# A bias table built in scratch memory: repeating the lines from on-chip memory, or from scratch memory itself

## The chip, the core and the metric

The kernel runs on one core of a Trainium2 chip. A core has TensorE (PE in the profile; its weight loads are PEld), VectorE (DVE), ScalarE (ACT), GpSimd (POOL) and SyncE (SP), each with an instruction stream of its own that it works off in order, and 16 DMA engines that carry the transfers which the others issue. SBUF is the on-chip memory of 128 partitions, PSUM the accumulators that PE writes. The metric is the device time of the whole program in microseconds (us).

## What is computed

One layer of a decoder trunk on 256 tokens of width 2048, in float32. The part that the change touches is the relative bias of the second head group:

```python
def reference(x, p, ln_mix_pre, w_in, ...):
    h = rms_norm(x, ln_mix_pre[i])
    q_sb, k_sb, v_sb, q_dl, k_dl, v_dl = split(h @ w_in[i])
    o_sb = stick_breaking_attention(q_sb, k_sb, v_sb)      # 8 heads
    o_dl = dilated_mixture(q_dl, k_dl, v_dl, rel_bias)     # 8 heads
    o = rms_norm(concat(o_sb, o_dl), ln_head[i])
    x = x + rms_norm(o @ w_out[i], ln_mix_post[i])
    g, u = split(rms_norm(x, ln_ffn_pre[i]) @ w_gate_up[i])
    x = x + rms_norm((silu(g) * u) @ w_down[i], ln_ffn_post[i])
    gate = sigmoid(rms_norm(x, ln_pli[i]) @ w_pli_gate[i])
    return x + gate * (p[i] @ w_pli_proj[i])

# in dilated_branch: logit[q, k] += rel_bias[t5_bucket(distance(q, k) * dilation)], per head
```

With 256 tokens the three dilations fold into one 128 x 256 bias per head that depends on query and key only by their distance: one line of 384 numbers per head, read one element further left in each row.

## The kernel before

Every large product is split in two float32r parts (`hi` and `lo`) and runs as three matmuls per 128 rows of weights, `hi*hi`, `hi*lo`, `lo*hi` (line 150). `load_w` brings 512 KB of weights at a time into one of four `wraw` buffers by a DMA that SyncE issues (line 99); ScalarE casts it to `whi` (line 104), VectorE takes the rest, `wlo` (line 105), both in five buffers. So weights are fetched several groups ahead, and a group is twelve matmuls on PE.

The attention works in four head groups of four: two of the stick-breaking kind, then two of the dilated kind. For each, `k`, `q` and `v` are projected (`project_T`, `project_v`); `project_T` evacuates (line 307), transposes on PE (line 312) into one of two `pt` accumulators, and ScalarE and VectorE split that into `kT` or `qT` (lines 318 and 319). The heads' own steps are put into the queue `pending`, one of which is written out per group of weights (`tick`): logits, sums, values (lines 353 to 355), `head_out` with a reciprocal root on POOL (`rsqrt`, line 201) and a scaling on VectorE (line 375), and the final transposes (line 380), which use the two `pt` accumulators as well. A scheduler puts the instructions of each engine into an order at build time; weights get a priority.

`load_bias` is called between the `k` and the `q` projection of the second stick group. A small matmul (line 471) and an addition (line 472) leave the eight lines in eight partitions of `line`, 384 numbers each. Line 474, on POOL's queue, writes each 128 times into `scratch` in DRAM; line 476 reads `scratch` back with a row step one element short, so that each row of `bias` is shifted by one. The first use of `bias` is line 438, in the first dilated group.

Of the kernel before, what the change touches and what calls it, by code (L numbers as in the profile page):

```python
# [10 lines left out]
F32 = mybir.dt.float32  # L11
# [5 lines left out]
P = 128  # L17
# [5 lines left out]
NH = 8  # L23
# [11 lines left out]
def kernel(  # L35
# [27 lines left out]
    nc = tc.nc  # L63
    x, p, w_in, w_out = x[0], p[0, 0], w_in[0], w_out[0]
    w_gate_up, w_down, w_pli_gate, w_pli_proj = w_gate_up[0], w_down[0], w_pli_gate[0], w_pli_proj[0]
    out = out[0]
# [4 lines left out]
    dram = ctx.enter_context(tc.tile_pool(name="dram", bufs=1, space=bass.MemoryType.DRAM))  # L71
# [53 lines left out]
    def later(fn, ready=lambda: True, first=False):  # L125
        (pending.appendleft if first else pending.append)((fn, ready))

    def after(n):
        at = clock[0] + n
        return lambda: clock[0] >= at  # L130
# [108 lines left out]
    with tc.tile_pool(name="mixed", bufs=1) as mixed:  # L239
# [46 lines left out]
        for j in (0, 2):  # L286
            nc.gpsimd.affine_select(
                out=zmask[:, j, :], in_=zmask[:, j, :], pattern=[[1, P]], base=-1, channel_multiplier=-1,
# [7 lines left out]
            out=tri[:, 0:P], in_=tri[:, 0:P], pattern=[[-1, P]], base=-1, channel_multiplier=1,  # L296
# [162 lines left out]
        def load_bias():  # L459

            oh = tmp.tile([P, 3 * P], F32, name="tmp")
            ac = tmp.tile([P, 3 * P], F32, name="tmp")
            line = tmp.tile([P, 3 * P], F32, name="tmp")
            rb = small.tile([32, NH], F32, name="rb", bufs=1)
            with tc.issue_after(mark[0]):
                nc.scalar.dma_start(out=oh[0:32], in_=onehot)
                nc.scalar.dma_start(out=rb, in_=rel_bias)
                nc.scalar.dma_start(out=ac[0:NH], in_=addc)
            def lines():
                pl = ps_a.tile([P, NB], F32, name="pa")  # L470
                nc.tensor.matmul(pl[0:NH, 0:384], lhsT=rb, rhs=oh[0:32], start=True, stop=True)
                nc.vector.tensor_tensor(line[0:NH], pl[0:NH, 0:384], ac[0:NH], ALU.add)
                scratch = dram.tile([NH, P, 384], F32, name="scratch")
                nc.gpsimd.dma_start(out=scratch, in_=line[0:NH].unsqueeze(1).broadcast_to([NH, P, 384]))
                skew = bass.AP(tensor=scratch.tensor, offset=scratch.offset + 127, ap=[[383, P], [P * 384, NH], [1, 2 * P]])
                nc.gpsimd.dma_start(out=bias, in_=skew)

            later(lines, after(4), first=True)
# [210 lines left out]
```

## Time and profile before

| | us |
|---|---|
| median of 3 runs (1289.17 to 1290.33) | 1289.73 |
| the profiled execution | 1289.67 |
| its span, first to last instruction | 1288.0 |
| PE busy in the span | 1264.1 (98%) |
| VectorE busy | 708.0 (55%) |
| ScalarE busy | 653.0 (51%) |
| POOL busy | 21.5 (2%) |

The span is what the profiler saw between the first and the last instruction; the execution's own time has 1.7 us more around it. Matmuls are pipelined and their ends are modelled, so PE's busy time says where it worked and not how well. A wait is put down to what released the engine last. A DMA's time to landing counts from its issue. The share of a DMA queue is the time of its packets over that of 16 engines in the stretch asked for.

### The profile page before, as it was taken

The numbers are of one execution on the slowest core, as the hardware profiler recorded it, in microseconds if no ns is written. First come the engines' busy times: TensorE is split into PE (matmuls) and PEld (weight loads), VectorE is DVE, ScalarE is ACT, GpSimd is POOL, SyncE is SP. The second block draws the span as 40 slices with busy tenths as digits, with TensorE's granted clock in tenths as the row PEclk, the third lists the DMA queues.
The fourth block names the chain that finished last, engine by engine and source line by source line (L and its number), as shares of the span: only waits on it lengthen the run. The fifth ranks groups of instructions, "written<-read, shape, count | busy, mean of one in ns | idle before, by whom it ended". The sixth has DMA issues, their size and how long they took to land.

```text
span 1288.0 us, 15227 instructions
## 1 busy us (share of the span) xinstructions
PE 1264.1 (98%) x5644; PEld 1018.6 (79%) x5644; DVE 708.0 (55%) x985; ACT 653.0 (51%) x1007; POOL 21.5 (2%) x39
## 2 busy tenths in 40 slices
PE   9999599999999999999999999999999999999998
PEld 6887488888888788888888888888888888887886
DVE  6575275555644755555555444455555545555754
ACT  7664255544543755555544334454554553445753
POOL 0001001000000000000000000000000000000000
PEclk9999799999999999999999999999999999999999
DMA  9856656555566666666666555666666665554662
GB/s 341 270 151 167 119 165 191 161 168 175 196 200 192 195 184 185 186 182 184 185 186 184 184 188 185 190 186 186 185 181 185 188 182 183 191 184 143 210 217 80
DMA packets 122811, 238.87 MB, mean 185 GB/s; under 512 B 7920, under 2 KB 8216, under 8 KB 122480
## 3 DMA queue, kind: packets, MB, share of 16 engines
q1 hardware_dynamic: 121360, 234.12, 59.0%
q0 software_dynamic: 1120, 3.67, 1.6%
q8 instruction: 44, 0.72, 0.2%
q14 instruction: 31, 0.25, 0.1%
q10 hardware_dynamic: 256, 0.10, 0.0%
HBM read 234.19 MB, written 3.67 MB: 185 GB/s over the span
## 4 chain that ended last, share of the span: by engine, by line
PE 96%; DMA 3%; DVE 0%; issue 0%; ACT 0%; POOL 0%; ACTq 0%; SPq 0%; DVEq 0%; POOLq 0%
PE pm L150 92%; DMA wraw<-in_w_in_dram 3%; PE pa L342 1%; PE pt L578 1%; PE pt L218 1%; PE pt L312 0%; PE pa L353 0%; PE pt L380 0%; PE pa L354 0%; PE pa L355 0%; PE pa L414 0%; ACT whi L104 0%; PE pt L450 0%; PE pa L416 0%; DVE wlo L105 0%
## 5 line engine op out<-in xcount | busy, mean ns | idle before, releaser
L150 PE MATMUL pm<-whi,hT_hi 128*128 128x512 f32 x1216 | 486.7, 400 | 0.8 <-ACT whi L104 0.8
L150 PE MATMUL pm<-whi,hT_lo 128*128 128x512 f32 x1216 | 481.7, 396 | 0.0
L150 PE MATMUL pm<-wlo,hT_hi 128*128 128x512 f32 x1216 | 481.3, 396 | 0.0
L110 DVE SCALAR_TENSOR_TENSOR wlo<-wraw,gT,whi 128x512 fp32r<-128x512 f32 x416 | 293.7, 748 | 242.9 <-ACT whi L109 242.7
L105 DVE TENSOR_TENSOR wlo<-wraw,whi 128x1024 fp32r<-128x1024 f32 (+1 forms) x222 | 269.8, 1216 | 276.0 <-ACT whi L104 275.3
L109 ACT ACTIVATE whi<-wraw,gT 128x512 fp32r<-128x512 f32 x416 | 278.6, 717 | 261.2 <-PE pm L150 258.2
L104 ACT CAST whi<-wraw 128x1024 fp32r<-128x1024 f32 (+1 forms) x222 | 231.2, 1042 | 313.7 <-PE pm L150 285.2
L150 PEld LDWEIGHTS pm<-whi,hT_hi 128*128 128x128 f32 x1216 | 228.7, 188 | 54.8 <-ACT whi L104 2.2
L150 PEld LDWEIGHTS pm<-whi,hT_lo 128*128 128x128 f32 x1216 | 228.4, 188 | 55.1
L150 PEld LDWEIGHTS pm<-wlo,hT_hi 128*128 128x128 f32 x1216 | 228.7, 188 | 53.0 <-DVE wlo L105 1.1
L150 PE MATMUL pm<-whi,fT_lo 128*128 128x512 f32 x352 | 139.4, 396 | 0.0
L150 PE MATMUL pm<-whi,fT_hi 128*128 128x512 f32 x352 | 139.4, 396 | 0.0
L150 PE MATMUL pm<-wlo,fT_hi 128*128 128x512 f32 x352 | 139.2, 396 | 0.0
L150 PEld LDWEIGHTS pm<-whi,fT_hi 128*128 128x128 f32 x352 | 66.1, 188 | 16.0
L150 PEld LDWEIGHTS pm<-wlo,fT_hi 128*128 128x128 f32 x352 | 66.1, 188 | 15.9
L150 PEld LDWEIGHTS pm<-whi,fT_lo 128*128 128x128 f32 x352 | 66.1, 188 | 15.9
L150 PE MATMUL pm<-whi,oT_hi 128*128 128x512 f32 x128 | 51.2, 400 | 0.0
L150 PE MATMUL pm<-whi,oT_lo 128*128 128x512 f32 x128 | 50.7, 396 | 0.0
L150 PE MATMUL pm<-wlo,oT_hi 128*128 128x512 f32 x128 | 50.6, 395 | 0.0
L150 PEld LDWEIGHTS pm<-whi,oT_lo 128*128 128x128 f32 x128 | 24.0, 188 | 5.7
L150 PEld LDWEIGHTS pm<-wlo,oT_hi 128*128 128x128 f32 x128 | 24.1, 188 | 5.5
L150 PEld LDWEIGHTS pm<-whi,oT_hi 128*128 128x128 f32 x128 | 24.1, 188 | 5.5
(119 smaller groups left out, 538.9 us busy)
## 6 DMA issues: line engine op xcount, KB each, us to landing
wraw<-in_w_gate_up_dram SPq DMA_DIRECT2D x176, 512.0 KB, 3.7
wraw<-in_w_in_dram SPq DMA_DIRECT2D x94, 512.0 KB, 3.8
wraw<-in_w_down_dram SPq DMA_DIRECT2D x88, 512.0 KB, 3.7
wraw<-in_w_out_dram SPq DMA_DIRECT2D x32, 512.0 KB, 3.7
wraw<-in_w_pli_gate_dram SPq DMA_DIRECT2D x32, 512.0 KB, 4.6
y_sb<-in_xT_dram SPq DMA_DIRECT2D x8, 256.0 KB, 6.7
y_sb<-in_x_dram SPq DMA_DIRECT2D x4, 512.0 KB, 7.5
x_sb<-in_x_dram SPq DMA_DIRECT2D x4, 512.0 KB, 6.5
```

What stands on the lines that cost most here:

```text
L104: nc.scalar.copy(hi[:, sl], raw[:, sl])
L105: nc.vector.tensor_tensor(lo[:, sl], raw[:, sl], hi[:, sl].bitcast(F32), ALU.subtract)
L109: nc.scalar.activation(out=hi[:, c], in_=raw[:, c], func=AF.Copy, scale=g)
L110: nc.vector.scalar_tensor_tensor(out=lo[:, c], in0=raw[:, c], scalar=g, in1=hi[:, c].bitcast(F32), op0=ALU.mult, op1=ALU.subtract)
L150: nc.tensor.matmul(self.pm[t], lhsT=a[:, g * KG + c, t, :], rhs=b[:, c, :], start=g == 0 and c == 0 and a is a_hi and b is hi, stop=g * KG ...
L218: nc.tensor.transpose(out=pt[:, k * P:(k + 1) * P], in_=x_sb[:, t, (c * 4 + k) * P:(c * 4 + k + 1) * P], identity=ident)
L342: nc.tensor.matmul(out, lhsT=a[u], rhs=b[w], start=i == 0, stop=i == 2)
L578: nc.tensor.transpose(out=pt[:, k * P:(k + 1) * P], in_=s[t][:, k * P:(k + 1) * P], identity=ident)
```

## The change

The eight lines are first written once to a small piece of DRAM, `lines_d` (12 KB). A second transfer reads `lines_d` 128 times into `scratch`, from DRAM to DRAM. `scratch` is laid out as 128 rows of eight lines instead of eight blocks of 128 rows, so that the repetition is the outermost dimension of both sides; the strides of the skewed read follow. All three transfers stand on POOL's queue, and each waits for the one before it to land.

```diff
-                scratch = dram.tile([NH, P, 384], F32, name="scratch")
-                nc.gpsimd.dma_start(out=scratch, in_=line[0:NH].unsqueeze(1).broadcast_to([NH, P, 384]))
-                skew = bass.AP(tensor=scratch.tensor, offset=scratch.offset + 127, ap=[[383, P], [P * 384, NH], [1, 2 * P]])
+                lines_d = dram.tile([1, NH * 384], F32, name="lines_d")
+                scratch = dram.tile([P, NH * 384], F32, name="scratch")
+                nc.gpsimd.dma_start(out=lines_d.rearrange("o (h i) -> (o h) i", h=NH), in_=line[0:NH])
+                nc.gpsimd.dma_start(out=scratch, in_=lines_d.broadcast_to([P, NH * 384]))
+                skew = bass.AP(
+                    tensor=scratch.tensor, offset=scratch.offset + 127,
+                    ap=[[NH * 384 - 1, P], [384, NH], [1, 2 * P]])
                 nc.gpsimd.dma_start(out=bias, in_=skew)
```

The new transfers change the order that the scheduler gives to some instructions; all that moves beside POOL's queue lies around the values of the second stick group. On POOL, from the last root of the first stick group on, before:

```order
L201 TENSOR_TENSOR rs_970<-d_968,mhalf 128x2
L474 DMA scratch<-tmp 1024x1x384
L201 TENSOR_TENSOR rs_1564<-d_1562,mhalf 128x2
L201 TENSOR_TENSOR rs_1596<-d_1594,mhalf 128x2
L476 DMA bias<-scratch 128x8x256
L201 TENSOR_TENSOR rs_1628<-d_1626,mhalf 128x2
L201 TENSOR_TENSOR rs_1660<-d_1658,mhalf 128x2
```

and after (`rs` are the roots of one head each, `d` what they are taken of; `tmp` is `line`):

```order
L201 TENSOR_TENSOR rs_970<-d_968,mhalf 128x2
L475 DMA lines_d<-tmp 8x384
L476 DMA scratch<-lines_d 128x3072
L480 DMA bias<-scratch 128x8x256
L201 TENSOR_TENSOR rs_1566<-d_1564,mhalf 128x2
L201 TENSOR_TENSOR rs_1598<-d_1596,mhalf 128x2
L201 TENSOR_TENSOR rs_1630<-d_1628,mhalf 128x2
L201 TENSOR_TENSOR rs_1662<-d_1660,mhalf 128x2
```

The read of `bias` has moved ahead of the first two of the group's four roots, and one DMA more stands there. On VectorE, behind the last addition of the second stick group's sums (line 417), the roots' users (line 375) and the sums under them (line 367), before:

```order
L367 TENSOR_SCALAR d_1562<-ssh 128x2
L105 TENSOR_TENSOR wlo<-wraw,whi 128x1024
L367 TENSOR_SCALAR d_1594<-ssh 128x2
L105 TENSOR_TENSOR wlo<-wraw,whi 128x1024 x4
L319 TENSOR_TENSOR kT<-pt,kT 128x4x128
L105 TENSOR_TENSOR wlo<-wraw,whi 128x1024
L319 TENSOR_TENSOR kT<-pt,kT 128x4x128
L375 TENSOR_SCALAR tmp<-pa,rs_1564 128x128 x2
L375 TENSOR_SCALAR tmp<-pa,rs_1596 128x128 x2
```

and after:

```order
L367 TENSOR_SCALAR d_1564<-ssh 128x2
L375 TENSOR_SCALAR tmp<-pa,rs_1566 128x128 x2
L105 TENSOR_TENSOR wlo<-wraw,whi 128x1024
L367 TENSOR_SCALAR d_1596<-ssh 128x2
L375 TENSOR_SCALAR tmp<-pa,rs_1598 128x128 x2
L105 TENSOR_TENSOR wlo<-wraw,whi 128x1024
L367 TENSOR_SCALAR d_1628<-ssh 128x2
L375 TENSOR_SCALAR tmp<-pa,rs_1630 128x128 x2
```

Each scaling now stands right behind the sum whose root it uses, one head after the other. On PE the values (lines 353 to 355) of the third and fourth of these heads, which stood side by side, have moved ahead accordingly, with twelve matmuls of line 150 between heads.

## Rows read from the trace of the kernel before

**Rows 1.** From the page: PE's busy time, granted clock and memory traffic in 40 slices.

```profile
PE 1264.1 (98%) x5644; PEld 1018.6 (79%) x5644; DVE 708.0 (55%) x985; ACT 653.0 (51%) x1007; POOL 21.5 (2%) x39
PEclk9999799999999999999999999999999999999999
GB/s 341 270 151 167 119 165 191 161 168 175 196 200 192 195 184 185 186 182 184 185 186 184 184 188 185 190 186 186 185 181 185 188 182 183 191 184 143 210 217 80
```

**Rows 2.** Waits of PE, whole span: who waited for whom, total us, times, longest.

```profile
PE pt L380 <- DVE qT L319: 15.6, 1, 15.6
PE pm L187 <- DVE junk L184: 1.3, 1, 1.3
```

**Rows 3.** Chain that ended last, 95 to 240 us: start, length, what.

```profile
106.91 0.22 PE pt L380 x2
...
127.66 28.71 DMA wraw<-in_w_in_dram
...
159.43 0.69 PE pt L380 x2
160.11 4.34 PE pm L150 x12
...
165.09 2.85 PE pm L150 x12
```

**Rows 4.** ScalarE's timeline, 127 to 160 us: start, length, what, [idle before <- releaser].

```profile
152.92 1.04 ACT L104 CAST whi<-wraw 128x1024 fp32r<-128x1024 f32 x1 [19.33 <-DMA wraw<-in_w_in_dram]
156.47 1.04 ACT L104 CAST whi<-wraw 128x1024 fp32r<-128x1024 f32 x1 [2.50 <-DMA wraw<-in_w_in_dram]
157.42 0.58 ACT L318 CAST qT<-pt 128x512 fp32r<-128x512 f32 x1
```

**Rows 5.** DMA issues, windows 117:120 (two rows), 127:130: count, KB, us to landing.

```profile
scratch<-tmp POOLq DMA_DIRECT2D x1, 1536.0 KB, 35.5
wraw<-in_w_in_dram SPq DMA_DIRECT2D x1, 512.0 KB, 3.7
...
wraw<-in_w_in_dram SPq DMA_DIRECT2D x1, 512.0 KB, 28.7
```

**Rows 6.** DMA queues, 123 to 152 us: packets, MB, share of 16 engines.

```profile
q0 software_dynamic: 667, 1.46, 47.0%
q1 hardware_dynamic: 879, 1.69, 18.1%
```

**Rows 7.** Busy time by engine, then PE's clock, DMA share, GB/s, behind the stall.

```profile
159.50:163.50 4.00, 4.00 (x11) 3.23 (x12) 3.13 (x4) 1.25 (x2) 0.00 (x0) 0.51 0.73 210
```

**Rows 8.** POOL's DMA queue and its one issue, 198 to 212 us.

```profile
q0 software_dynamic: 272, 1.05, 23.1%
...
bias<-scratch POOLq DMA_DIRECT2D x1, 1024.0 KB, 8.5
```

**Rows 9.** Memory traffic in 40 slices and POOL's DMA queue, 427 to 440 us (`gpost`).

```profile
GB/s 0 0 0 0 0 328 76 302 403 454 403 429 328 403 233 113 214 372 422 290 69 0 0 0 0 0 0 0 0 0 0 95 82 88 277 410 410 208 44 88
...
q0 software_dynamic: 144, 1.05, 22.5%
```

**Rows 10.** POOL's timeline, 110 to 240 us.

```profile
119.95 1.28 POOL L474 DMA_DIRECT2D scratch<-tmp  x1 [13.31 <-DVE tmp L472]
194.45 0.71 POOL L201 TENSOR_TENSOR rs<-d,mhalf 128x2 f32<-128x2 f32 x1 [73.22 <-DVE d L367]
...
198.54 0.95 POOL L476 DMA_DIRECT2D bias<-scratch  x1
```

**Rows 11.** A small DMA load, from the list of issues.

```profile
rb<-in_rel_bias_dram ACTq DMA_DIRECT2D x1, 1.0 KB, 2.4
```

**Rows 12.** First use of `bias`, VectorE's timeline, 185 to 245 us.

```profile
239.95 0.29 DVE L438 CUSTOM_DVE_ANT_0 tmp<-pa,bias 128x128 f32<-128x128 f32 x1 [1.02 <-PE pa L342]
```

**Rows 13.** Waits of VectorE, 100 to 350 us.

```profile
DVE wlo L105 <- ACT whi L104: 87.5, 59, 19.7
...
DVE tmp L375 <- POOL rs L201: 8.1, 11, 0.9
```

## The prediction

> **What bounds the kernel now.** I read the page first. The granted clock is at its upper level in all slices but one, and the engine that is nearly always busy is TensorE (PE), so a gain has to be found where PE stands still or runs at the lower clock [rows 1]. Then the waits of PE over the whole span: one stands out, 15.6 us before the transposes of line 380, put down to VectorE's `qT` of line 319; the next longest is 1.3 us [rows 2]. Then the chain of waits in that stretch, to see what stood behind VectorE. It is a weight load: issued at 127.66 us, landed 28.71 us later, at 156.37, and the transposes follow at 159.43 [rows 3]. The link between them is ScalarE, which works in order: its evacuation of `qT` (157.42) stood queued behind two casts, at 152.92 and 156.47, whose weights had not landed; the first had waited 19.33 us [rows 4].
>
> Why did the weights not land? The load issued between 117 and 120 us lands in 3.7 us, the one issued between 127 and 130 takes 28.7 us. What lies between is the repetition of the bias lines, `scratch<-tmp`, issued at 119.95 and 35.5 us under way [rows 5, 10]. While it ran (123 to 152 us), its queue held 47.0% of the 16 DMA engines' time, which is 7.5 engines busy without a break, and the weights got 18.1% [rows 6]. Its source is 8 partitions of SBUF, each read 128 times, and 7.5 of 16 fits eight engines with one head each. A weight load lies on all sixteen and is not there until its last engine has delivered; so eight clogged engines delay every load.
>
> The Trainium skill, "DMA: Bandwidth & Descriptors", section "Rules for kernel authors", says that an outermost dimension smaller than 16 confines a transfer to at most that many engines. The 47.0% agrees with it.
>
> PE's stop also has an echo: the page's clock row dips in the stall's own slice, the fifth [rows 1], and in the four microseconds in which PE works again the granted clock is 0.51 [rows 7]. That is the lower level, 1.2 GHz, after a stretch in which PE did nothing.
>
> **The change part by part.**
>
> *What goes.* The stall of 15.6 us [rows 2]. The lower clock behind it: the two transposes took 0.69 us and take 0.22 elsewhere, twelve matmuls took 4.34 and the next twelve 2.85, so 0.47 + 1.49 = 2.0 us [rows 3]. Together 17.6 us, if no new wait takes the place.
>
> *How much delay the loads bear.* The load on the chain landed at 156.37 and PE lost 15.6 us, so it may land as late as 156.37 - 15.6 = 140.8 and cost nothing. It is issued at 127.66 and lands in 3.7 us when nothing is in its way, at 131.4. So 9.4 us of delay are free; each further microsecond costs PE one. The load ahead of it bears more in the same way.
>
> *The first hop.* The 12 KB go out by a transfer of their own: about 1 us of issue on POOL, which does nothing from 120 to 194 us [rows 10], and a landing that I bound by the 1 KB load, 2.4 us, and by the 1 MB load that POOL issues, 8.5 us [rows 8, 11]. It is nearer to the small one; the repetition is issued at some 123 instead of 120 us. Nobody waits for the `bias` before the additions at 239.95 us [rows 12], so the hop costs nothing on PE.
>
> *The repetition itself.* Memory to memory is not in this trace. What counts is how long it holds each engine, S, because a load can be delayed by at most that. Three rows bound it, each spread over 16 engines. The `gpost` load reads one line of 8 KB 128 times from memory: 22.5% of 13 us is 2.9 us for 1.05 MB, so 4.4 us for 1.57 MB [rows 9]. The `bias` load, read in 1 KB runs: 23.1% of 14 us is 3.2 us, so 4.8 [rows 8]. The old repetition: 47.0% of 29 us is 13.6 us for 1.46 MB, so 14.7 for all of it [rows 6]. I take 4.6, near the first two: the new source is memory, a line of 12 KB read 128 times, which is what `gpost` does; only the target differs. Then the load lands at 131.4 + 4.6 = 136.0, 4.8 us early. At 14.7 it lands at 146.1, 5.3 us late.
>
> *The `bias` load.* It moves from 198.54 us to right behind the repetition, around 133. There it meets a prefetch that has lost ground. If all its 3.2 us fell before the same load, that would land at 139.2, still 1.6 us early. Where it stands now it costs PE nothing either: no wait of PE but the stall is over 1.3 us, and its 8.5 us make none [rows 2, 8]. So moving it gives and costs 0, as long as S is below 6 us; beyond that it comes after the load in question.
>
> *What the move holds up on POOL.* The order puts both new DMAs and the `bias` DMA ahead of all four reciprocal roots of the second stick group, and POOL waits in order for the repetition to land. The first of the four ran at 194.45 [rows 10], with the stall gone at 176.9. Even a repetition that takes 35.5 us from 123 is done at 159. So nothing waits; it would only do so from a repetition of over 53 us.
>
> *The new order on VectorE and PE.* Each head's scaling (line 375) now follows its root directly, and the products of heads 2 and 3 stand with twelve matmuls between them instead of side by side. VectorE then waits up to 0.9 us for each root, as it does now, with the next `wlo` queued behind: 4 x 0.9 = 3.6 us at worst, but VectorE waits for ScalarE's casts (87.5 - 19.7) / 58 = 1.2 us at each `wlo` of that stretch anyway [rows 13]. The instructions on PE are the same in number. I take 0, with 0.3 us either way.
>
> **Sum.** The profiled execution took 1289.67 us (span 1288.0), the median of the runs is 1289.73; the two agree. 1289.67 - 15.6 - 2.0 = 1272.1.
>
> **The rivals.**
>
> *A smaller stall stays.* Two mechanisms end in this. The repetition keeps its pace per byte but over 16 engines: S = 14.7, 5.3 us late, 1277.4, or 1279.4 if the lower clock comes back with it. Or memory carries it twice, read and write: 3.15 MB beside weights at 185 GB/s. The best slices that the trace shows are 454 GB/s in one of a third of a microsecond [rows 9] and 341 in one of the page's forty [rows 1], so S is 3.15/(454 - 185) = 11.7 us or 3.15/(341 - 185) = 20.2 us, the load lands 2.3 or 10.8 us late, and the time is 1274.4 to 1282.9, with the clock 1284.9. For it speaks that the target is memory too; against it that 454 GB/s passed for reading alone without a sign of a limit.
>
> The Trainium skill, "HBM Reference", section "Specifications (TRN2)", gives about 358 GB/s per core. By it S would be an estimated 18.2 us and the time some 1281 to 1283; the 454 GB/s of the trace speak against so low a limit for a core that runs alone.
>
> *It doesn't spread, and is slower.* If the repetition stays on eight engines at the old pace, everything is as before but starts a hop later: 1.28 us of issue and 2.4 of landing [rows 10, 11]. The load then lands at 160.1, the stall is 19.3 us and the time 1293.4. More generally, the kernel is slower from the point where S passes 156.37 - 131.4 = 25 us. For it: the eight engines are my reading of a share, not a row that names them. Against it: in the new transfer 128 is the outermost size on both sides.
>
> *No change*: S happens to lie between 22 and 28 us. No row points there.
>
> **How the numbers follow.** I give the forecast 0.62, the smaller stall 0.26 (0.10 for the old pace over 16 engines, 0.16 for memory that carries it twice), no change 0.05, slower 0.07. A measurement of this kernel tells some 0.2% from no change, 2.6 us; both of the first two cases but for a sliver are faster by more. So faster 0.88, same 0.05, slower 0.07. The range: from 1271.0 (the 0.3 us of the order and a little for a stall removed more fully) up to 1279.8, which takes in S = 14.7 with its clock and about two thirds of the smaller-stall case: 0.62 + 0.17 = 0.79.
>
> **What would show it.** Right: PE's wait before line 380 is gone; the loads issued from 124 to 130 us land in under 13 us; the clock's row has no dip in the fifth slice; the two new queue entries land by about 135 us, and `bias` is issued then. S can be read as the share of POOL's queue times the length of its window. Wrong: loads that still take over 13 us, with PE idle behind them (then S is what I mis-sized); or POOL's roots late around 177 us and PE waiting behind line 375; or a new wait of PE between 135 and 150 us with the `bias` load beside it.

## The result, and the profile after

| | before | after |
|---|---|---|
| median of 4 runs each, us | 1289.76 | 1271.37 (1271.30 to 1271.86) |
| ratio, 95% interval | | 0.9858 (0.9841 to 0.9875) |
| span of the profiled execution, us | 1288.0 | 1269.7 |
| PE busy | 1264.1 (98%) | 1261.5 (99%) |

The kernel is 18.4 us faster; 17.6 were forecast, 1272.1 us, and the range of 1271.0 to 1279.8 holds the time. The page of the kernel after, for [rows 1]: the clock's row has no dip any more.

```profile
PE 1261.5 (99%) x5644; PEld 1017.2 (80%) x5644; DVE 708.7 (56%) x985; ACT 652.8 (51%) x1007; POOL 21.5 (2%) x40
PEclk9999999999999999999999999999999999999999
```

Waits of PE in the whole span, for [rows 2]. The 15.6 us before line 380 are gone, and what was second is now first:

```profile
PE pm L187 <- DVE junk L184: 1.3, 1, 1.3
PE pm L150 <- DVE wlo L105: 0.5, 1, 0.5
```

POOL's timeline, for [rows 10]: the hop, the repetition, the read of `bias`, and the first root of the second stick group.

```profile
119.47 0.71 POOL L475 DMA_DIRECT2D lines_d<-tmp  x1 [13.30 <-DVE tmp L472]
121.73 0.57 POOL L476 DMA_DIRECT2D scratch<-lines_d  x1 [1.54 <-DMA lines_d<-tmp]
132.10 0.93 POOL L480 DMA_DIRECT2D bias<-scratch  x1 [9.81 <-DMA scratch<-lines_d]
176.43 0.71 POOL L201 TENSOR_TENSOR rs<-d,mhalf 128x2 f32<-128x2 f32 x1 [43.40 <-DVE d L367]
```

The DMA issues, for [rows 5]: the three of POOL, and the two weight loads issued as the repetition began, at 123.95 us (window 122 to 124) and 127.17 us (window 127 to 130).

```profile
scratch<-lines_d POOLq DMA_DIRECT2D x1, 1536.0 KB, 10.1
...
bias<-scratch POOLq DMA_DIRECT2D x1, 1024.0 KB, 9.1
...
lines_d<-tmp POOLq DMA_DIRECT2D x1, 12.0 KB, 2.0
...
wraw<-in_w_in_dram SPq DMA_DIRECT2D x1, 512.0 KB, 9.0
...
wraw<-in_w_in_dram SPq DMA_DIRECT2D x1, 512.0 KB, 7.3
```

The loads beside the repetition now take 7 to 9 us instead of 28. The repetition held POOL's queue for this share of the 16 engines in 122 to 132 us:

```profile
q0 software_dynamic: 144, 1.57, 49.6%
```

Share times 16 engines times length of the window is the engine time, what a single engine would need for all packets: 0.496 x 16 x 10 = 79 us, 5.0 us on each of 16. For the kernel before the same row over 121 to 156 us is

```profile
q0 software_dynamic: 704, 1.58, 42.1%
```

which is 0.421 x 16 x 35 = 236 us of engine time for as many bytes. The start and length of each packet in the two traces bear out the number of engines that the prediction read from a share: before, up to eight packets of the repetition are under way at once (eight for 20.2 us, nine for less than 0.1); after, up to sixteen (more for 0.2 us). So the engines were not only fewer, each of them was three times as slow. The prediction had this pace only as an upper bound of S (14.7 us against 4.4 and 4.8) and did not ask where it comes from; the experiments below do.

### The profile page after: what moved, and what is told of

Its sections match the earlier page's. It is cut to its first block, busy times and chain, and to the rows that moved or that the text cites. A ratio compares the mean times of both kernels' runs of the same rounds, so it can differ in the third digit from the quotient of the medians.

```text
span 1269.7 us, 15227 instructions
## 1 busy us (share of the span) xinstructions
PE 1261.5 (99%) x5644; PEld 1017.2 (80%) x5644; DVE 708.7 (56%) x985; ACT 652.8 (51%) x1007; POOL 21.5 (2%) x40
## 3 DMA queue, kind: packets, MB, share of 16 engines
HBM read 235.76 MB, written 3.68 MB: 189 GB/s over the span
## 4 chain that ended last, share of the span: by engine, by line
PE 98%; DMA 1%; DVE 0%; issue 0%; ACT 0%; POOL 0%; ACTq 0%; DVEq 0%; POOLq 0%
PE pm L150 94%; PE pa L342 1%; PE pt L582 1%; PE pt L218 1%; PE pt L312 1%; DMA wraw<-in_w_in_dram 0%; DMA gT<-in_gains_dram 0%; PE pa L353 0%; PE pa L354 0%; PE pa L355 0%; PE pt L380 0%; PE pa L414 0%; PE pt L450 0%; PE pa L416 0%; DVE wlo L105 0%
```

## The experiments

Each run was timed against the kernel before on the same chip. Each row of POOL's DMA queue (packets, MB, share of 16 engines) is asked for from before the repetition's first packet to behind its last.

### Memory to memory, but with 8 outermost

```diff
-                scratch = dram.tile([P, NH * 384], F32, name="scratch")
+                scratch = dram.tile([NH, P, 384], F32, name="scratch")
-                nc.gpsimd.dma_start(out=scratch, in_=lines_d.broadcast_to([P, NH * 384]))
+                nc.gpsimd.dma_start(
+                    out=scratch,
+                    in_=lines_d.rearrange("o (h i) -> (o h) i", h=NH).unsqueeze(1).broadcast_to([NH, P, 384]))
```

(The strides of the skewed read go back to those of the kernel before.)

> Memory to memory as in the changed kernel, but scratch laid out as eight blocks of 128 rows again, so that 8 is the outermost size of the repetition. POOL's order is the old one here (bias behind two roots). The changed kernel takes 1271.4 us; its repetition has 128 packets of 12 KB. If the spread over 16 engines alone made the gain (eight engines at the old pace, S = 29 us), the stall is back: 1288 to 1294. If what was slow is the reading of one SBUF partition per engine, the new pace on eight engines gives S = 2 x 4.9 = 9.9 us, the load lands 0.5 us too late at most, and the time is 1271.4 to 1273. If the new order of the roots made the gain, it is lost with the old order: 1289.

Measured: 1271.43 us (1271.10 to 1271.93), as fast as the changed kernel. POOL's queue, 122 to 136 us:

```profile
q0 software_dynamic: 704, 1.58, 30.6%
```

0.306 x 16 x 14 = 69 us of engine time, 8.6 us on each of eight engines, where the second theory has 9.9. So 128 as the outermost dimension, the part of the change that looked like its core, is not needed for the gain. And the order of the roots isn't either: in this run `bias` is read at 180.33 us, behind two of the roots, as before.

### From SBUF, but from 128 partitions

```diff
-                nc.tensor.matmul(pl[0:NH, 0:384], lhsT=rb, rhs=oh[0:32], start=True, stop=True)
-                nc.vector.tensor_tensor(line[0:NH], pl[0:NH, 0:384], ac[0:NH], ALU.add)
+                nc.vector.tensor_copy(
+                    rb16.rearrange("b (h r) -> b h r", r=16), rb.unsqueeze(2).broadcast_to([32, NH, 16]))
+                nc.tensor.matmul(pl[:, 0:384], lhsT=rb16, rhs=oh[0:32], start=True, stop=True)
+                nc.vector.tensor_tensor(line, pl[:, 0:384], ac, ALU.add)
...
-                nc.gpsimd.dma_start(out=scratch, in_=line[0:NH].unsqueeze(1).broadcast_to([NH, P, 384]))
+                nc.gpsimd.dma_start(
+                    out=scratch.rearrange("h (r j) i -> (h r) j i", j=8),
+                    in_=line.unsqueeze(1).broadcast_to([P, 8, 384]))
```

(`ac` is loaded with 16 copies of each line.)

> No hop and no memory source: the matmul of the lines makes 16 copies of each line in 128 partitions (its left side is widened), and one transfer from SBUF writes each partition eight times. So 16 engines, source SBUF as before. If the spread is what counts and the pace of the SBUF source is better too with 8 partitions per engine, S is about 5 us and the time 1271.4, or a little less. If the old pace per engine stays (14.7 us on each of 16), the load lands 5.3 us late: 1276.7, with the clock up to 1278.7.

Measured: 1271.61 us (1271.01 to 1272.35). POOL's queue, 119 to 127 us, and the repetition's landing, without a hop ahead of it:

```profile
q0 software_dynamic: 368, 1.57, 53.7%
...
scratch<-tmp POOLq DMA_DIRECT2D x1, 1536.0 KB, 7.8
```

0.537 x 16 x 8 = 69 us again. So SBUF as a source is not slow in itself, and the detour through memory is not needed either. What both runs share, against the kernel before, is that the repeated reading doesn't go to partitions 0 to 7 alone.

### The slack: the repetition done twice and three times

```diff
+                for i in range(2):
+                    spare = dram.tile([P, NH * 384], F32, name=f"spare{i}")
+                    nc.gpsimd.dma_start(out=spare, in_=lines_d.broadcast_to([P, NH * 384]))
                 nc.gpsimd.dma_start(out=scratch, in_=lines_d.broadcast_to([P, NH * 384]))
```

(`range(1)` for twice.)

> The changed kernel with the repetition done twice (the first into a spare piece of memory that nobody reads), back to back. By the slack of 9.4 us: S = 2 x 4.9 = 9.9 us, the load lands 0.5 us late, 1271.4 to 1272. If the slack was overestimated and the 4.9 us are already at its edge: a stall of some 5 us, 1276. If engines' time is not what delays the loads (for example the hop or a port that the sources share), nothing changes: 1271.4.

> The same with three repetitions. By the slack: S = 14.9 us, 5.5 us late, a stall of some 5.5 us and 1277, up to 1279 if the clock falls with it. If engines' time is not what delays the loads: 1271.4.

Measured: 1272.01 us (1271.35 to 1273.20) with two, 1279.58 (1279.18 to 1279.81) with three. With two the load issued at 127.05 us lands after 13.1 us and PE waits 0.8 us for its weights. With three the old stall is back in small. Waits of PE, whole span, of the kernel with three repetitions:

```profile
PE pt L380 <- DVE qT L319: 5.9, 1, 5.9
PE pm L187 <- DVE junk L184: 1.3, 1, 1.3
```

and its chain, 115 to 165 us:

```profile
126.78 19.07 DMA wraw<-in_w_in_dram
...
148.90 0.69 PE pt L380 x2
149.59 4.56 PE pm L150 x12
...
154.78 2.85 PE pm L150 x12
```

5.5 us of stall were expected and 5.9 came; the clock adds (0.69 - 0.22) + (4.56 - 2.85) = 2.2 us, and 5.9 + 2.2 = 8.1 is nearly all of the 8.2 us between 1271.4 and 1279.6. So the term "9.4 us of delay are free, each further one costs PE one" holds. Three repetitions also move three times the bytes in memory, so by themselves they don't show that the loads wait for engines and not for memory. The kernel before shows that: there the loads waited longest, while all queues together moved 107 GB/s (122 to 154 us).

### Which eight partitions: 0, 4 to 28; 0, 2 to 14; 0, 16 to 112

The transfer of the kernel before, SBUF to memory, eight engines, one source partition each. Only the step between the partitions differs; the matmul makes as many copies of each line as the step says, and one of them is read (here 4; in the other two runs 2 and 16).

```diff
-                nc.gpsimd.dma_start(out=scratch, in_=line[0:NH].unsqueeze(1).broadcast_to([NH, P, 384]))
+                nc.gpsimd.dma_start(
+                    out=scratch, in_=line[0:32:4].unsqueeze(1).broadcast_to([NH, P, 384]))
```

> The transfer of the kernel before, eight engines and SBUF as source, no hop; only the eight source partitions are no longer 0 to 7 but 0, 4, 8 to 28 (the matmul makes four copies of each line and every fourth partition is read). In the run e1_mem8 a packet of 4608 B from memory took 191 ns on eight engines, in the kernel before 681 ns from partitions 0 to 7. If it was slow because one engine reads one partition over and over, nothing changes: 681 ns a packet, 1290. If it was slow because neighbouring partitions are read through one port, these eight have a port each: about 200 ns, S = 8.6 to 9.9 us, 1271.4 to 1272.

> The same with source partitions 0, 2, 4 to 14. If one partition per engine is what is slow: 1290, 681 ns a packet. If ports of four neighbouring partitions are: four ports instead of two, so half of 681, 340 ns a packet, S = 14.6 us on eight engines; the load lands 0.5 to 5.3 us late, 1272 to 1279.

> The same with source partitions 0, 16, 32 to 112. If only the distance between them counts, this is the best of the three: 200 ns, 1271.4 to 1272. By the port table of the Trainium skill, SBUF - State Buffer, Door 1, these eight lie on four ports, as those of e6_step2 do: an estimated 340 ns a packet and the time of e6_step2.

Measured: 1271.76 us (1271.19 to 1272.88) with a step of 4, 1273.70 (1272.76 to 1274.36) with 2, 1274.24 (1273.20 to 1275.72) with 16. POOL's queue with a step of 4, 122 to 136 us:

```profile
q0 software_dynamic: 704, 1.58, 28.9%
```

with a step of 2, 121 to 139 us:

```profile
q0 software_dynamic: 704, 1.58, 37.8%
```

and with a step of 16, 122 to 141 us:

```profile
q0 software_dynamic: 704, 1.58, 37.8%
```

In engine time 65, 109 and 115 us, where partitions 0 to 7 took 236. It isn't that one engine reads one partition over and over, for that is so in all four. It isn't the distance either, for a step of 16 is no better than one of 2. What fits is that neighbouring partitions share a way out, a port: with a step of 1 the eight sources lie in two groups of four neighbours, with a step of 2 in four, with a step of 4 in eight, and the first doubling of the groups doubles the pace, the second makes it 1.7 times as fast again. By its pace a step of 16 counts as four groups, so partitions far apart would share a port as well; that was foretold from the table named next, and no run here tries a single pair of them.

The Trainium skill, "SBUF — State Buffer", section "Door 1: The DMA port swizzle", gives the table: partitions 0 to 3 on one port, 4 to 7 on another, and of 0, 16 to 112 always two on one. It puts a port at 27.2 GB/s. The measured rates agree: 1.58 MB in 29.5 us of eight engines is 54 GB/s on two ports, in 14.4 us 110 GB/s on four (step of 16). With eight ports it is 195 GB/s in 8.1 us, about what eight engines do from memory (8.6 us), so there the ports need no longer be the limit.

### Sixteen engines on neighbouring partitions

```diff
+                nc.gpsimd.dma_start(
+                    out=scratch.rearrange("h (r j) i -> (h r) j i", j=64),
+                    in_=line[0:16].unsqueeze(1).broadcast_to([16, 64, 384]))
```

(Two copies of each line, in partitions 0 to 15, in place of the transfer of the kernel before.)

> Sixteen engines, but neighbouring sources: two copies of each line in partitions 0 to 15, each written 64 times, 16 the outermost size. If engines were the limit (14.7 us of each at the old pace of 681 ns) or if four ports are (two engines share what one had: again 681 ns), S is 14.7 us on all 16 and the load lands 4 to 5.3 us late: 1275 to 1279. If 16 engines alone help: 200 ns a packet, 1271.4.

Measured: 1276.93 us (1275.89 to 1278.98). POOL's queue, 122 to 140 us, and the repetition's landing:

```profile
q0 software_dynamic: 368, 1.57, 81.8%
...
scratch<-tmp POOLq DMA_DIRECT2D x1, 1536.0 KB, 19.2
```

0.818 x 16 x 18 = 236 us of engine time: twice the engines, and the pace of each is the old one. That the four ports set it, and not a pace that each engine has on neighbours, follows from the step of 2: the same four ports and half the engines, 116 GB/s there and 107 here.

It is also the slowest of the three runs with four ports. The first load behind the repetition (window 120 to 122 us) is held up here, and was not with a step of 2 (second line) or of 16 (5.1 us):

```profile
wraw<-in_w_in_dram SPq DMA_DIRECT2D x1, 512.0 KB, 17.5
...
wraw<-in_w_in_dram SPq DMA_DIRECT2D x1, 512.0 KB, 5.0
```

The load after it takes 17.3 us here, 15.2 with a step of 2 and 15.5 with 16. And the clock falls again, to 0.61 in 142 to 146.4 us. From the chains of this run and of the one with a step of 16, the twelve matmuls behind the stall:

```profile
142.01 4.34 PE pm L150 x12
...
146.16 2.79 PE pm L150 x12
```

From the matmul of the lines to the first logits behind the stall these two profiled executions (1278.98 and 1274.06 us) differ by 2.4 us: PE waits 3.1 us instead of 2.1, and the twelve matmuls take 1.5 us more. The other 2.5 us lie outside that stretch, 1.25 of them ahead of it. Why the first load is held up was not tried apart: all sixteen engines are taken here, where eight were left to the weights, and the repetition's first packet comes 1.5 us behind its issue instead of 3.3 or 3.4.

The ports of the table are by the Trainium skill's page named above; the time of the kernel before is that of the first comparison.

| sources of the repetition | engines | ports | engine time, us | us per engine | time, us |
|---|---|---|---|---|---|
| SBUF 0 to 7 (before) | 8 | 2 | 236 | 29.5 | 1289.8 |
| SBUF 0 to 15 | 16 | 4 | 236 | 14.7 | 1276.9 |
| SBUF 0, 16 to 112 | 8 | 4 | 115 | 14.4 | 1274.2 |
| SBUF 0, 2 to 14 | 8 | 4 | 109 | 13.6 | 1273.7 |
| SBUF 0, 4 to 28 | 8 | 8 | 65 | 8.1 | 1271.8 |
| memory, 8 outermost | 8 | - | 69 | 8.6 | 1271.4 |
| SBUF 0 to 127 | 16 | 16 | 69 | 4.3 | 1271.6 |
| memory, 128 outermost (after) | 16 | - | 79 | 5.0 | 1271.4 |

From 8.6 us per engine on down the time no longer follows: the loads' slack hides it all, and no median got below the changed kernel's. Above that, engine time alone doesn't set the time either: 13.6 to 14.9 us per engine (with the run of three repetitions) cost between 2.3 and 8.2 us.

## Why the prediction was right, and where its reason was not

**What bounds the kernel, and the sum: right.** The load that waits behind the repetition, the casts in ScalarE's queue, the `qT` behind them and PE behind that were the chain. Between the matmul of the lines and the first logits after the stall, the piece of the chain that holds stall and clock, before took 164.45 - 118.32 = 46.1 us and after 146.38 - 117.85 = 28.5. The difference is 17.6, the forecast. The two ends in the chain before:

```profile
118.32 0.74 PE pa L471 x2
...
164.45 0.64 PE pa L342 x6
```

The chain of the kernel after, 95 to 240 us, runs there on PE alone:

```profile
117.85 0.74 PE pa L471 x2
...
143.36 0.22 PE pt L380 x2
143.58 2.81 PE pm L150 x12
146.38 0.64 PE pa L342 x6
```

and the clock is at its upper level in the stretch where it was 0.51 [rows 7]:

```profile
159.50:163.50 4.00, 4.00 (x20) 3.36 (x19) 3.72 (x7) 2.75 (x5) 0.00 (x0) 1.00 0.47 131
```

The 0.7 us beyond the forecast lie elsewhere: 0.5 at the very start (the matmul of the lines begins at 117.85 instead of 118.32, ahead of all that was changed), the rest spread behind; runs of one kernel differ by as much.

**The terms.** The hop landed in 2.0 us (2.4 taken) and the repetition was issued at 121.73 (123). S was 5.0 us (4.6), the load issued as it began took 9.0 us (3.7 + 4.6 = 8.3), under the 13 that it may. `bias` was read from 132.10 on (133), and no wait of PE came of it. The first root ran at 176.43 (176.9). The new order of VectorE's scalings cost nothing, as forecast: up to the dilated logits the two kernels differ by 18.1 us, as they did ahead of it by 18.1 at the first stick logits, and the longest wait for a root is 0.9 us as before [rows 13] (10.4 us in 13 waits, 8.1 in 11 before, over 100 to 350 us):

```profile
DVE tmp L375 <- POOL rs L201: 10.4, 13, 0.9
```

The slack came out best of all. The load on the chain may take 3.7 + 9.4 = 13.1 us. With a step of 2, with a step of 16 and with three repetitions it took 13.46, 15.27 and 19.07, so it was 0.4, 2.2 and 6.0 us late, and PE waited 0.3, 2.1 and 5.9 us for it. Load and wait with a step of 2, then of 16:

```profile
126.52 13.46 DMA wraw<-in_w_in_dram
...
PE pt L380 <- DVE qT L319: 0.3, 1, 0.3
...
127.39 15.27 DMA wraw<-in_w_in_dram
...
PE pt L380 <- DVE qT L319: 2.1, 1, 2.1
```

S is a rougher measure of the delay than "at most S" has it. With three repetitions S was 14.9 us and the delay 19.07 - 3.7 = 15.4, above it; with a step of 16 S was 14.4 and the delay 11.6, below it; that load was issued 4.4 us behind the repetition's first packet.

**The step that failed** is the reading of the 47.0% [rows 6]. It was right that eight engines were busy without a break, and wrong that the number eight was why. The Trainium skill's rule on the outermost dimension ("DMA: Bandwidth & Descriptors", section "Rules for kernel authors") agreed with the row, and I took agreement for the cause. The row itself said more: 1.46 MB in 13.6 us of 16 engines is a third of the pace of `bias` [rows 8] and `gpost` [rows 9], per engine, and a count of engines doesn't explain a pace per engine. The forecast survived since it took the new pace from the loads from memory; the count of sixteen added nothing to it, for at that pace eight engines cost nothing either.

**Two rivals fell with it.** "It doesn't spread, and is slower" was priced at 1293.4, for eight engines at the old pace. Eight engines with memory as a source give 1271.4: had the transfer not spread, nothing would have been lost. And "the old pace on 16 engines", 1277.4 to 1279.4, does exist, but belongs to neighbouring partitions: with 16 engines on partitions 0 to 15 it came out at 1276.9.

**Memory that carries the repetition twice** set no limit: S was 5.0 us, not 11.7 to 20.2. All DMA and POOL's queue in 123 to 131 us, in which the whole repetition passed:

```profile
DMA packets 455, 2.17 MB, mean 271 GB/s; under 512 B 37, under 2 KB 37, under 8 KB 327
...
q0 software_dynamic: 141, 1.57, 62.0%
```

What is read is 2.17 MB, and 1.57 MB of it are written to memory again: 3.74 MB in 8 us, 467 GB/s in and out. (The page of the profile counts 1.57 MB more read from memory than before, 235.76 against 234.19, so each repeated read is in this figure.) The Trainium skill, "HBM Reference", section "Specifications (TRN2)", had about 358 GB/s per core, and says below its table that a core which streams alone goes well above that share. The measured rate agrees with the second: for this core, running alone, the 358 was no bound.

## What to carry to other kernels

When a transfer holds a share of the DMA engines for long, divide twice: how many engines, and what pace each; the second points at the source, the first at the shape. Lines that are to be repeated many times by DMA should not stand in neighbouring partitions: spread them over partitions of different ports (here a step of 4 was enough), or repeat from memory. And a transfer that nobody waits for can still stop the kernel by what it does to the prefetch beside it; its price is what it delays the prefetch's loads by, less their slack. Engine time gives that delay only roughly, and doing the transfer two and three times measures the slack.

## What was not expected

- The pace of an engine depends on which SBUF partitions the others read beside it: 236 us of engine time for 1.58 MB from partitions 0 to 7, 65 us for as much from 0, 4 to 28, on eight engines both times.
- More engines need not help: sixteen on four ports gave 1276.9 us, eight on four ports 1273.7 and 1274.2.
- A repetition from memory in rows of 12 KB leaves little room beside it: the load issued as it began landed 9.0 us later, about its own 3.8 and the 5.0 of the whole repetition, as if queued behind it. In 124 to 127 us POOL's queue moved 68 packets and the weights' queue none. Whether the long rows or the source make it so was not tried.
